# Probabilities of three attentions split to fp16 and turned by DMA; gate projections of the second layer moved ahead

## The chip, the cores and the metric

One of the eight cores of a Trainium2 chip runs the kernel. TensorE multiplies (the stationary operand is loaded first, the moving one streams past it) and writes PSUM; VectorE (DVE), ScalarE (ACT) and GpSimd (POOL) work on rows of 128 partitions; DMA queues move data between HBM and SBUF, or within SBUF. All DMAs of this kernel are issued in order from one queue, SyncE's (SP). The metric is the time of one execution on the device in microseconds; lower is better.

## What is computed

Two layers of a transformer trunk on a sequence of 1024 tokens with 1024 features. Each layer normalises `x`, projects it, runs two attentions, gates their outputs with `silu` of a gate projection, and projects back with a residual.

```python
def layer_ab(x, ...):            # A: top-256 of causal keys by an indexer; B: window of 128 with sinks
    oa = dsa_attention(qa, ka, va, qi, ki, wi, k_sel)
    ob = swa_sink_attention(qb, kb, vb, b_sinks)
    return x + concat([oa * silu(za), ob * silu(zb)]) @ w_out

def layer_cd(x, ...):            # C: compressed + selected + window 512, mixed by gates; D: latent attention
    oc = nsa_attention(qc, kc, vc, ks, vs, kw, vw, gates, n_sel)
    q  = (rms_norm(cq,  d_q_lat_norm)  @ d_w_uq)
    kv = (rms_norm(ckv, d_kv_lat_norm) @ d_w_ukv)
    od = mla_attention(q_nope, q_rope, k_nope, k_rope, kv_v)
    return x + concat([oc * silu(zc), od * silu(zd)]) @ w_out

def masked_softmax(s, mask):     # in every attention, before p @ v
    p = exp(s - max(s)); return p / sum(p)
```

Every attention has 8 heads in two groups of 4. A is the masked one: its mask comes from the top-k search.

## The kernel before

The sequence is cut into 8 blocks of 128 tokens. Products that need float32 accuracy are made from split operands: a high part and the rest, so that one product takes three matmuls (high x high, high x low, low x high). A projection chunk (`fill_gen`) is 256 columns of weights or a little more: for each of 8 blocks 8 x 3 matmuls (L490 to L492) run into a PSUM bank `pp`, and `post` evacuates it. Weights come by SP, ScalarE and GpSimd split them into `whi` and `wlo` (L446, L447); of the 14 buffer pairs a chunk uses 8, so 6 tiles are fetched ahead.

`attn_gen` runs a list of jobs, one for each block `i` and head group `g`. For `nk` keys, 4, 2 or 1 heads share one tile `pt` of up to 1024 columns: scores on TensorE into `psS` (L636), mask and running minimum of the negated scores on VectorE (L639), `exp` on ScalarE with the minimum `nm` as bias (L644). Then `tstage`, for four blocks of 128 columns at a time: TensorE turns the blocks (L664) into the PSUM tile `psT`, and the turned float32 probabilities are scaled by 4096 and split into two fp16 tiles `ph` and `pl`. The table `WAYS` says how, by attention and head group: in way `p` ScalarE writes `ph` (L668) and VectorE `pl` (L669), in way `q` ScalarE copies to `sg` (L673) and GpSimd does both (L674, L675). `cstage` multiplies with the values: three matmuls for each block (L682 to L684) into `po`; this is called P.V here. Transposes and P.V lag behind the scores by `tlag` groups.

C runs three kinds of jobs for each block and group (compressed keys `kcs`, selected `ks`, window `kw`), 52 tiles `pt` in a head group with 280 blocks of 128 columns; its first 24 jobs are head group 0, the next group 1. D has 44 tiles with 288 blocks, B 16 tiles with 120, A 44 tiles with 288.

`Lanes.run` interleaves a main list (attention) with a fill (projections): for each unit of cost that the main list yields, the fill may yield a ratio of it (`CR` for C, `DR` for D). The fill of C is the string `FOO`, the chunks of the second layer in order, followed by `d_prologue`, which prepares D: weights, keys, the first queries. `cq` (query latents) waits until group 0 of C is done. What the generators yield is the program's order; a scheduler then sets the final order of each engine.

Buffers that the steps touch: `pt` 3, `ph` and `pl` 4 each of four blocks, `sg` 2, `xr` (the residual of the last projection) 2, `wraw2` (raw weights of D and of the last projection) 2.

Of the kernel before, what the change touches and what calls it, by code (L numbers as in the profile page):

```python
# [38 lines left out]
PSCALE = 4096.0  # L39
SLOT = 2048  # L40
# [3 lines left out]
CR = 0.75  # L44
DR = 0.8
WB = 2
XB = 2
# [6 lines left out]
FOO = 'ks kc kw qc0 zc0 zc1 cq qc1 zd0 zd1 ck'  # L54
# [108 lines left out]
def trunk(ctx: ExitStack, tc: tile.TileContext, A, out):  # L163
# [165 lines left out]
    def tps():  # L329
        return psT.tile([P, 4, P], F32, name="psT")  # L330
# [202 lines left out]
    def v_scale(m, res):  # L533

        yield from L.take_in("psT", PTC)
        ps = tps()
        T.transpose(ps[0:1, 0], m, identf)
        yield
        r = st.tile([P, 2], F32, name="vs_r")
        V.tensor_reduce(r[0:1, 0:1], ps[0:1, 0], AX.X, OP.max)  # L540
        V.tensor_scalar(r[0:1, 0:1], r[0:1, 0:1], 2.0 ** -90, None, op0=OP.max)
        yield
        T.matmul(ps[:, 1, 0:1], r[0:1, 0:1].to_broadcast([1, P]), identf[0:1, 0:1], start=True, stop=True)
        yield
# [43 lines left out]
    def attn_gen(jobs):  # L588
# [9 lines left out]
        for jb in jobs:  # L598
# [22 lines left out]
            for h0 in range(0, 4, per):  # L621
# [33 lines left out]
                for c in range(0, len(todo), 4):  # L655
# [3 lines left out]
                    def tstage(jb=jb, grp=grp, pt=pt, lastg=lastg, vh=vh, vl=vl, nk=nk, get_po=get_po, fin=fin, cmp_=cmp_,  # L659
                               fb=fbox if h0 + per == 4 else None):  # L660
# [6 lines left out]
                        if next(jb["way"]) == "p":  # L667
                            S.activation(ph[:, :n], pT[:, :n], AF.Copy, scale=PSCALE)  # L668
                            V.scalar_tensor_tensor(pl[:, :n], pT[:, :n], PSCALE, ph[:, :n], op0=OP.mult,  # L669
                                                   op1=OP.subtract)  # L670
                        else:
                            sg = wk.tile([P, 4, P], F32, name="sg", bufs=SG)
                            S.activation(sg[:, :n], pT[:, :n], AF.Copy, scale=PSCALE)  # L673
                            G.tensor_scalar(ph[:, :n], sg[:, :n], 1.0, 1.0, op0=OP.mult, op1=OP.mult)  # L674
                            G.tensor_tensor(pl[:, :n], sg[:, :n], ph[:, :n], OP.subtract)  # L675
# [13 lines left out]
                        return cstage, n * 110  # L689
# [633 lines left out]
    def lat_pre():  # L1323
# [5 lines left out]
        B["glat"] = cc.tile([P, 384], F32, name="glat")  # L1329
        nc.sync.dma_start(B["glat"][:, 0:256], row(A["d_q_lat_norm"][0], 0, 256))  # L1330
        nc.sync.dma_start(B["glat"][:, 256:384], row(A["d_kv_lat_norm"][0], 0, 128))
# [3 lines left out]
    def lat_chain(z, ss, n, g, dst):  # L1335
# [3 lines left out]
        V.scalar_tensor_tensor(z, z, r[0], g, op0=OP.mult, op1=OP.mult)  # L1339
# [10 lines left out]
    def lat_start(ps, n, g, dst):  # L1350
# [5 lines left out]
        L.post(lat_chain(z[:, :n], ss, n, g, dst))  # L1356

    def cq_post(i, ps):
        t = slice(i * P, (i + 1) * P)
        lat_start(ps, 256, B["glat"][:, 0:256], (B["cqh"][:, :, t], B["cql"][:, :, t]))  # L1360
# [5 lines left out]
    def ck_post(i, ps):  # L1366
        t = slice(i * P, (i + 1) * P)
        lat_start(ps[:, 0:128], 128, B["glat"][:, 256:384], (B["ckh"][:, None, t], B["ckl"][:, None, t]))
# [78 lines left out]
    def small_w(ap, rows, n, tag):  # L1447
# [90 lines left out]
    def next_query():  # L1538
# [4 lines left out]
        if (i, g) == (0, 0):  # L1543
            D["wuq", 1] = small_w(wq[:, 384:768], 2, 384, "q")

    def d_prologue():
# [4 lines left out]
        D["wuq", 0] = small_w(wq[:, 0:384], 2, 384, "q")  # L1551
        D["wkv", 0] = small_w(wkv[:, 0:512], 1, 512, "kv")
        B["vscd"] = []
        L.post(v_bound(wkv, 1, B["glat"][:, 256:384], [], B["vscd"], ("vscd",)))
# [179 lines left out]
    D["wkv", 1] = small_w(wkv[:, 512:1024], 1, 512, "kv")  # L1734
# [63 lines left out]
```

## Time and profile before

| | us |
|---|---|
| three runs, median (lowest to highest) | 1560.41 (1559.73 to 1562.62) |
| the profiled execution | 1559.19 |
| its span, first to last instruction | 1557.4 |
| busy: TensorE, VectorE, ScalarE, GpSimd | 1384.3, 1226.1, 869.8, 821.4 |
| DMA: moved, busy share of the 16 engines | 93.19 MB, 20% |

The stages, by where the score matmuls of each attention stand in the trace: indexer scores to 168 us, B from 170 to 430, A from 428 to 636 (P.V included), projections alone to 839, C from 839 to 1226 (group 0 to 1038), D from 1264 to 1537, the last of the output after that. Shares over the whole span are means over stages with different limits, so the profile is read stage by stage: which engine is busy nearly all the time there, and which waits. A TensorE that is listed as busy may still hold a slow stream; its granted clock stands beside it.

### The profile page before, as it was taken

The page shows a single profiled execution, that of the slowest core. Times are in us where ns is not written, and L with a number is a line of the kernel's source. Part 1 is how long each engine was busy: PE and PEld are TensorE (multiplying, and loading weights), DVE is VectorE, ACT ScalarE, POOL GpSimd, SP SyncE. Part 2 cuts the span into 40 slices and gives each one's busy share as a digit, 9 for nine tenths or more (in the row PEclk, how much of TensorE's full clock was granted, in tenths as well). Part 3 has the DMA queues.
Part 4 walks back from the last instruction along what each step waited for, and adds up shares of the span by engine and source line. Part 5 has one row for each costly group of instructions (what it writes and reads, how often), then busy time and mean ns, then how long its engine had stood idle before and what let it go on. Part 6 is the DMA issues. An engine that isn't in the chain of part 4 may idle for free.

```text
span 1557.4 us, 35155 instructions
## 1 busy us (share of the span) xinstructions
PE 1384.3 (89%) x12588; PEld 1273.9 (82%) x12588; DVE 1226.1 (79%) x3827; ACT 869.8 (56%) x2385; POOL 821.4 (53%) x1097
## 2 busy tenths in 40 slices
PE   6998888788637889999999999999999778889999
PEld 6888878788636779999999998899988556778887
DVE  8599999999998876428338668976689999996763
ACT  6354576577406766325424666956667666754531
POOL 4767642467777657324447343565456565652240
PEclk9999999989867999999999999999999879989999
DMA  6311212111102132332312210012100210111232
GB/s 199 86 35 32 57 56 71 43 36 33 45 17 69 59 107 76 111 108 86 82 36 55 66 49 8 9 47 63 33 15 19 78 62 15 32 55 59 95 112 75
DMA packets 88431, 93.19 MB, mean 60 GB/s; under 512 B 20928, under 2 KB 73152, under 8 KB 88256
## 3 DMA queue, kind: packets, MB, share of 16 engines
q1 hardware_dynamic: 88256, 90.95, 19.3%
q8 instruction: 99, 1.62, 0.4%
q14 instruction: 76, 0.62, 0.1%
HBM read 67.85 MB, written 23.07 MB: 58 GB/s over the span
## 4 chain that ended last, share of the span: by engine, by line
PE 48%; DVE 33%; DMA 6%; POOL 5%; issue 5%; ACT 3%; SPq 0%; POOLq 0%; DVEq 0%; ACTq 0%
PE psS L636 8%; PE pp L490 7%; PE pp L492 6%; PE pp L491 6%; PE psT L664 6%; DVE junk L845 6%; DVE pt L639 4%; PE pp L1683 2%; PE pp L1681 2%; PE pp L1682 2%; PE po L684 2%; PE po L682 2%; PE po L683 2%; DMA wraw<-in_ab_w_in 1%; POOL wlo L447 1%
## 5 line engine op out<-in xcount | busy, mean ns | idle before, releaser
L490 PE MATMUL pp<-whi,Rh 128*128 128x256 f32 (+4 forms) x1648 | 489.1, 297 | 25.9 <-DVE zst L581 9.9
L492 PE MATMUL pp<-whi,Rl 128*128 128x256 f32 (+4 forms) x1648 | 481.0, 292 | 0.6 <-DVE Rl L327 0.6
L491 PE MATMUL pp<-wlo,Rh 128*128 128x256 f32 (+4 forms) x1648 | 480.0, 292 | 0.0
L490 PEld LDWEIGHTS pp<-whi,Rh 128*128 128x128 f32 x1648 | 322.5, 196 | 33.1 <-DVE zst L581 13.9
L644 ACT ACTIVATE pt<-pt,nm 128x256 f32<-128x256 f32 (+8 forms) x384 | 246.6, 643 | 178.6 <-DVE nm L639 173.3
L492 PEld LDWEIGHTS pp<-whi,Rl 128*128 128x128 f32 x1648 | 321.1, 195 | 2.2 <-DVE Rl L327 1.1
L491 PEld LDWEIGHTS pp<-wlo,Rh 128*128 128x128 f32 x1648 | 322.0, 196 | 1.0
L447 POOL TENSOR_TENSOR wlo<-wraw,whi 128x256 fp32r<-128x256 f32 (+4 forms) x208 | 162.3, 787 | 189.6 <-ACT whi L446 176.9
L664 PE MATMUL psT<-identf,pt 128*128 128x128 f32 x1256 | 216.1, 284 | 14.2 <-DVE pl L669 4.2
L674 POOL TENSOR_SCALAR ph<-sg 128x512 f16<-128x512 f32 (+3 forms) x157 | 89.3, 570 | 157.9 <-ACT sg L673 142.0
L664 PEld LDWEIGHTS psT<-identf,pt 128*128 128x128 f32 x1256 | 147.3, 143 | 28.1 <-issue 4.3
L675 POOL TENSOR_TENSOR pl<-sg,ph 128x512 f16<-128x512 f32 (+3 forms) x157 | 163.4, 1041 | 8.7
L446 ACT ACTIVATE whi<-wraw 128x256 fp32r<-128x256 f32 (+4 forms) x208 | 83.7, 416 | 125.0 <-DMA wraw<-in_cd_w_in 37.8
L669 DVE SCALAR_TENSOR_TENSOR pl<-psT,ph 128x512 f16<-128x512 f32 (+3 forms) x233 | 128.4, 556 | 26.8 <-ACT ph L668 26.4
L668 ACT ACTIVATE ph<-psT 128x512 f16<-128x512 f32 (+3 forms) x233 | 111.9, 492 | 51.7 <-PE psT L664 49.2
L684 PEld LDWEIGHTS <-pl 128*128 128x128 f16 x1256 | 114.2, 99 | 26.1 <-issue 7.4
L682 PEld LDWEIGHTS <-ph 128*128 128x128 f16 x1256 | 116.7, 100 | 20.0 <-issue 7.9
L683 PEld LDWEIGHTS <-ph 128*128 128x128 f16 x1256 | 116.7, 100 | 14.7 <-issue 13.5
L639 DVE CUSTOM_DVE_ANT_0 pt<-psS,mk 128x512 f32<-128x512 f32 (+4 forms) x208 | 107.1, 518 | 23.7 <-PE psS L636 21.8
L673 ACT ACTIVATE sg<-psT 128x512 f32<-128x512 f32 (+3 forms) x157 | 83.4, 534 | 32.7 <-PE psT L664 30.1
L344 POOL TENSOR_TENSOR nz<-nz,rs_y 128x512 f32<-128x512 f32 (+2 forms) x44 | 41.2, 937 | 94.0 <-DVE rs_y L288 68.2
L636 PE MATMUL psS<-ka,qs 128*128 128x512 f32 (+4 forms) x192 | 58.7, 405 | 24.1 <-DVE nm L639 23.8
(311 smaller groups left out, 3622.4 us busy)
## 6 DMA issues: line engine op xcount, KB each, us to landing
wraw<-in_cd_w_in SPq DMA_DIRECT2D x72, 128.0 KB, 2.1
wraw<-in_ab_w_in SPq DMA_DIRECT2D x56, 128.0 KB, 2.2
xs<-in_x SPq DMA_DIRECT2D x8, 512.0 KB, 6.0
od<-mx SPq DMA_DIRECT2D x32, 128.0 KB, 1.8
wraw<-in_ab_w_out SPq DMA_DIRECT2D x32, 128.0 KB, 2.2
x<-in_x SPq DMA_DIRECT2D x8, 512.0 KB, 4.6
mo<-od SPq DMA_DIRECT2D x16, 256.0 KB, 2.7
nz<-zdr SPq DMA_DIRECT2D x16, 256.0 KB, 2.8
```

What stands on the lines that cost most here:

```text
L447: G.tensor_tensor(lo[:, :o], raw[:, :o], hi[:, :o].bitcast(F32), OP.subtract)
L490: T.matmul(ps, xh, hi[:, :n], start=q == 0 and k == 0, stop=False)
L491: T.matmul(ps, xh, lo[:, :n], start=False, stop=False)
L492: T.matmul(ps, xl, hi[:, :n], start=False, stop=q == 3 and k == 1)
L636: T.matmul(ps[:, at + a - c:at + b - c], lhs, rhs(a, b), start=n == 0, stop=n == len(pl_) - 1)
L639: V.tensor_tensor_reduce(pt[:, j * nk + c:j * nk + c + w], ps[:, at:at + w], mask(c, w), -1.0, first, op0=OP.add, op1=OP.min, accum_out=low)
L644: S.activation(pt[:, j * nk:(j + 1) * nk], pt[:, j * nk:(j + 1) * nk], AF.Exp, scale=-1.0, bias=nm[:, h:h + 1], accum_out=sm[:, h:h + 1])
L664: T.transpose(pT[:, a], pt[:, o:o + P], identf)
L675: G.tensor_tensor(pl[:, :n], sg[:, :n], ph[:, :n], OP.subtract)
L682: T.matmul(dst, ph[:, a], vh(kt, h), start=kt == 0, stop=False)
L683: T.matmul(dst, ph[:, a], vl(kt, h), start=False, stop=False)
L684: T.matmul(dst, pl[:, a], vh(kt, h), start=False, stop=kt == nt - 1)
```

## The change

For B, C and D, `WAYS` now has the ways `g` and `d`, chosen once for a tile `pt`. The tile is split before it is turned: ScalarE copies it to fp16 (`hl`, first half), VectorE (`d`) or GpSimd (`g`) writes the rest into the second half, and one DMA on SP turns all blocks of both halves into `ht`, from which P.V takes its stationary operands. `hl` and `ht` have two buffers each. In A the ways `p` and `q` stay, chosen by tile too, and write into `ht`. The factor 4096 moves into the bias of `exp`: one more small ScalarE instruction on `nm` for each tile. In `FOO` the gate projections zd0 and zd1 move ahead of cq and qc1, and `CR` goes from 0.75 to 1.5; a turned tile's `tstage` counts 1 instead of 110 a block in the main list's cost. Besides, the latent norms' gains are multiplied into D's weights instead of the latents, and `xr` shares the two buffers of `wraw2`.

```diff
-CR = 0.75
+CR = 1.5
-XB = 2
-FOO = 'ks kc kw qc0 zc0 zc1 cq qc1 zd0 zd1 ck'
+FOO = 'ks kc kw qc0 zc0 zc1 zd0 zd1 cq qc1 ck'
+HLB = 2
+HTB = 2
-PHB = 4
-SG = 2
-WAYS = ('q', 'q', 'ppq', 'pq', 'ppq', 'pq', 'ppq', 'p')
+WAYS = ('g', 'g', 'ppq', 'pq', 'dg', 'dg', 'dgg', 'dg')
...
+                S.activation(nm[:, h0:h0 + per], nm[:, h0:h0 + per], AF.Copy, bias=LNP)
                 for j, h in enumerate(hs):
                     S.activation(pt[:, j * nk:(j + 1) * nk], pt[:, j * nk:(j + 1) * nk], AF.Exp, scale=-1.0,
                                  bias=nm[:, h:h + 1], accum_out=sm[:, h:h + 1])
+                way = next(jb["way"])
+                nb = per * nk // P
+                hts = []
+
+                def get_ht(hts=hts):
+                    if not hts:
+                        hts.append(wk.tile([P, 16, P], F16, name="ht", bufs=HTB))
+                    return hts[0]
+
+                if way in "dg":
+                    n = nb * P
+                    hl = wk.tile([P, 2048], F16, name="hl", bufs=HLB)[:, :2 * n]
+                    S.activation(hl[:, :n], pt[:, :n], AF.Copy)
+                    (V if way == "d" else G).tensor_tensor(hl[:, n:], pt[:, :n], hl[:, :n], OP.subtract)
+                    nc.sync.dma_start(get_ht()[:, :2 * nb], hl.rearrange("p (k n) -> p k n", n=P), transpose=True)
...
-                        pT = tps()
-                        for a, (h, kt, o) in enumerate(grp):
-                            T.transpose(pT[:, a], pt[:, o:o + P], identf)
-                        ph = wk.tile([P, 4, P], F16, name="ph", bufs=PHB)
-                        pl = wk.tile([P, 4, P], F16, name="pl", bufs=PHB)
...
+                        ht = get_ht()
+                        ph, pl = ht[:, c:c + n], ht[:, nb + c:nb + c + n]
+                        if way in "pq":
+                            pT = tps()
+                            for a, (h, kt, o) in enumerate(grp):
+                                T.transpose(pT[:, a], pt[:, o:o + P], identf)
...
-                        return cstage, n * 110
+                        return cstage, n * 110 if way in "pq" else 1
...
+            S.activation(raw, raw, AF.Copy, scale=B["glat"][:, g + r:g + r + 1])
...
-            xr = D["pool"].tile([P, 512], F32, name="xr", bufs=XB)
+            xr = D["pool"].tile([P, 512], F32, name="xr", tag="wraw2", bufs=WB)
```

How this moves instructions is shown at three places.

On TensorE, around the last scores of C (`kw`). Before, transposes of `pt` and the key projection of D (`whkv`, `wlkv`) stand around them:

```order
L664 MATMUL psT<-identf,pt 128x128 x2
L682 LDWEIGHTS ph
L682 MATMUL po<-vhs,ph 128x64
L683 LDWEIGHTS ph
L683 MATMUL po<-vls,ph 128x64
L1498 MATMUL pp<-whkv,Rh 128x256
L1499 MATMUL pp<-wlkv,Rh 128x256
L1500 MATMUL pp<-whkv,Rl 128x256
L636 MATMUL psS<-kw_10951,qs 128x320 x2
```

After (line numbers are those of the changed file):

```order
L699 LDWEIGHTS ht
L699 MATMUL po<-vhs,ht 128x64
L700 LDWEIGHTS ht
L700 MATMUL po<-vls,ht 128x64
L701 LDWEIGHTS ht
L701 MATMUL po<-vhs,ht 128x64
L637 MATMUL psS<-kw_10635,qs 128x320 x4
L637 MATMUL psS<-kd_16888,qhl 128x512 x2
L637 MATMUL psS<-krs,qrs 128x512
```

The transposes are gone, the operands of P.V come from `ht`, and the first scores of D (`kd`, `krs`) follow the last ones of C at once: the key projection for them stands earlier.

On SP, where the last projection chunk of C (160 columns, `ck`) is loaded. Before, the stores of gate projections (`zst`) are still going on:

```order
L442 DMA wraw<-in_cd_w_in 128x160 x3
L582 DMA zdr_102<-zst 128x256
L442 DMA wraw<-in_cd_w_in 128x160
L1295 DMA od_101<-cacc 128x256
L442 DMA wraw<-in_cd_w_in 128x160 x2
L582 DMA zdr_102<-zst 128x256
L442 DMA wraw<-in_cd_w_in 128x160 x2
```

After:

```order
L662 DMA_TRANSPOSE ht<-hl 128x16x128 x4
L662 DMA_TRANSPOSE ht<-hl 128x10x128 x2
L443 DMA wraw<-in_cd_w_in 128x160 x2
L662 DMA_TRANSPOSE ht<-hl 128x10x128 x2
L443 DMA wraw<-in_cd_w_in 128x160 x4
L1312 DMA od_101<-cacc 128x256
L443 DMA wraw<-in_cd_w_in 128x160
```

The gate stores stand earlier, as their chunks do, and transposing DMAs of 16 and 10 blocks stand between the loads.

On VectorE, near the beginning of D (`kd`, `krs`, `vdl`: keys and values of D). Before, `pl` comes in pieces of 512 columns for most tiles:

```order
L1488 TENSOR_TENSOR krs<-psT,krs 64x256
L639 ISA pt,nm<-psS,mk,nm_20436 128x384
L639 ISA nm 128x1
L669 SCALAR_TENSOR_TENSOR pl<-psT,ph 128x512
L278 TENSOR_SCALAR rs_y<-rs_v 128x8
L281 TENSOR_TENSOR rs_t<-rs_t,rs_v 128x8
L669 SCALAR_TENSOR_TENSOR pl<-psT,ph 128x512
L639 ISA pt,nm_20516<-psS,mk 128x512
L639 ISA nm_20516 128x1
```

After:

```order
L640 ISA pt,nm_19046<-psS,mk 128x512
L640 ISA nm_19046 128x1
L640 ISA pt,nm<-psS,mk,nm_19046 128x384
L640 ISA nm 128x1
L574 SCALAR_TENSOR_TENSOR vdl<-pp,vs_e,vdh 128x128 x2
L661 TENSOR_TENSOR hl<-pt,hl 128x1024
L640 ISA pt,nm_19113<-psS,mk 128x512
L640 ISA nm_19113 128x1
L574 SCALAR_TENSOR_TENSOR vdl<-pp,vs_e,vdh 128x128 x2
```

One subtraction of a whole tile (`hl`, 1024 columns) stands there for one tile, and none for its neighbours, whose way is `g`.

## Rows read from the trace of the kernel before

**Rows 1.** Busy time by stretch: its length, each engine (instructions), clock, DMA.

```profile
core 0: us, PE busy (x) PEld busy (x) DVE busy (x) ACT busy (x) POOL busy (x), PEclk, DMA share, GB/s
92.00:428.00 336.00, 276.72 (x2238) 263.15 (x2237) 328.49 (x937) 199.53 (x551) 195.14 (x245) 0.92 0.16 44
...
839.00:1038.00 199.00, 196.75 (x2136) 184.61 (x2135) 151.30 (x571) 131.24 (x386) 95.09 (x130) 1.00 0.14 38
1038.00:1203.00 165.00, 160.50 (x1782) 152.43 (x1782) 129.03 (x534) 107.86 (x340) 94.84 (x135) 1.00 0.11 32
1203.00:1264.00 61.00, 40.08 (x336) 32.63 (x335) 58.16 (x224) 39.21 (x118) 34.02 (x51) 0.78 0.22 68
1264.00:1400.00 136.00, 115.53 (x1011) 97.57 (x1011) 128.32 (x392) 92.19 (x237) 83.97 (x106) 0.91 0.14 43
1400.00:1557.00 157.00, 153.80 (x1177) 128.42 (x1175) 97.04 (x270) 61.74 (x152) 39.94 (x52) 1.00 0.26 85
```

**Rows 2.** Timeline of TensorE: start, duration, line, operands, count.

```profile
1132.89 0.93 PE L664 MATMUL psT<-identf,pt 128*128 128x128 f32 x7
1133.57 0.54 PE L636 MATMUL psS<-kw,qs 128*128 128x320 f32 x2
```

**Rows 3.** Busy time by stretch of the transposes alone (L664).

```profile
92.00:428.00 336.00, 22.79 (x120) 14.57 (x120) 0.92 0.16 44
839.00:1264.00 425.00, 97.17 (x560) 65.29 (x560) 0.97 0.14 40
1264.00:1400.00 136.00, 26.34 (x160) 18.89 (x160) 0.91 0.14 43
1400.00:1557.00 157.00, 20.76 (x130) 14.83 (x128) 1.00 0.26 85
```

**Rows 4.** Timeline of TensorE, last scores of C and first of D.

```profile
1225.48 0.45 PE L636 MATMUL psS<-kw,qs 128*128 128x320 f32 x2
1225.78 0.28 PE L1498 MATMUL pp<-whkv,Rh 128*128 128x256 f32 x1
1225.90 0.28 PE L1499 MATMUL pp<-wlkv,Rh 128*128 128x256 f32 x1
...
1264.12 1.91 PE L636 MATMUL psS<-kd,qhl 128*128 128x512 f32 x4
```

**Rows 5.** Busy time by stretch of VectorE's `pl` alone (L669).

```profile
1038.00:1264.00 226.00, 24.55 (x47) 0.94 0.14 42
1264.00:1400.00 136.00, 18.31 (x31) 0.91 0.14 43
1400.00:1557.00 157.00, 23.94 (x41) 1.00 0.26 85
```

**Rows 6.** Groups by shape: count, busy us, mean ns, idle before.

```profile
L516 DVE SCALAR_TENSOR_TENSOR pt<-x,rs_y,gx 128x1024 f32<-128x1024 f32 x8 | 10.3, 1294 | 0.2
L510 ACT ACTIVATE pt<-x 128x1024 f32<-128x1024 f32 x8 | 8.5, 1059 | 1.7 <-DVE x L1091 1.7
L675 POOL TENSOR_TENSOR pl<-sg,ph 128x512 f16<-128x512 f32 x38 | 44.6, 1175 | 2.7
L715 ACT ACTIVATE es<-es 128x4 f32<-128x4 f32 x16 | 3.1, 196 | 4.2 <-DVE es L713 4.2
```

**Rows 7.** Busy time by stretch of VectorE's gates alone (L581).

```profile
1038.00:1264.00 226.00, 6.61 (x16) 0.94 0.14 42
```

**Rows 8.** DMA issues: operands, count, KB each, us to landing.

```profile
mo<-od SPq DMA_DIRECT2D x16, 256.0 KB, 2.7
x1d<-x SPq DMA_DIRECT2D x8, 512.0 KB, 3.0
xs<-in_x SPq DMA_DIRECT2D x8, 512.0 KB, 6.0
rope<-in_c_rope SPq DMA_DIRECT2D x1, 256.0 KB, 7.5
```

**Rows 9.** Waits of SP's queue: us in total, times, longest.

```profile
SPq L442 <- POOL wlo L447: 363.3, 160, 27.8
```

More of the change, by code (lines that the diff above doesn't have):

```diff
@@ L39 @@
 PSCALE = 4096.0
+LNP = float(np.log(PSCALE))
+HLB = 2
+HTB = 2
 SLOT = 2048
@@ L657, in attn_gen, with tstage @@
                     lastg = h0 + per == 4 and c + 4 >= len(todo)
-                    def tstage(jb=jb, grp=grp, pt=pt, lastg=lastg, vh=vh, vl=vl, nk=nk, get_po=get_po, fin=fin, cmp_=cmp_,
-                               fb=fbox if h0 + per == 4 else None):
+                    def tstage(grp=grp, pt=pt, lastg=lastg, vh=vh, vl=vl, nk=nk, get_po=get_po, fin=fin, cmp_=cmp_,
+                               fb=fbox if h0 + per == 4 else None, way=way, get_ht=get_ht, nb=nb, c=c):
                         n = len(grp)
-                        pT = tps()
-                        for a, (h, kt, o) in enumerate(grp):
-                            T.transpose(pT[:, a], pt[:, o:o + P], identf)
-                        ph = wk.tile([P, 4, P], F16, name="ph", bufs=PHB)
-                        pl = wk.tile([P, 4, P], F16, name="pl", bufs=PHB)
[L667 to L675, printed above, removed]
@@ new lines, in tstage @@
+                        ht = get_ht()
[4 more added lines that the diff above has]
+                                T.transpose(pT[:, a], pt[:, o:o + P], identf)
+                        if way == "p":
+                            S.activation(ph, pT[:, :n], AF.Copy)
+                            V.tensor_tensor(pl, pT[:, :n], ph, OP.subtract)
+                        elif way == "q":
+                            sg = wk.tile([P, 4, P], F32, name="sg", tag="hl", bufs=HLB)
+                            S.activation(sg[:, :n], pT[:, :n], AF.Copy)
+                            G.tensor_scalar(ph, sg[:, :n], 1.0, 1.0, op0=OP.mult, op1=OP.mult)
+                            G.tensor_tensor(pl, sg[:, :n], ph, OP.subtract)
@@ L1328, in lat_pre, with lat_chain @@
         D["kx"] = ks_[:, 1024:2048].rearrange("p (a b n) -> p a b n", a=2, b=2)
-        B["glat"] = cc.tile([P, 384], F32, name="glat")
-        nc.sync.dma_start(B["glat"][:, 0:256], row(A["d_q_lat_norm"][0], 0, 256))
-        nc.sync.dma_start(B["glat"][:, 256:384], row(A["d_kv_lat_norm"][0], 0, 128))
+        B["glat"] = cc.tile([P, 3], F32, name="glat")
+        nc.sync.dma_start(B["glat"][:, 0:2], A["d_q_lat_norm"][0].rearrange("(k p) -> p k", p=P))
+        nc.sync.dma_start(B["glat"][:, 2:3], A["d_kv_lat_norm"][0].rearrange("(k p) -> p k", p=P))
         G.tensor_scalar(B["glat"], B["glat"], RG, 1.0, op0=OP.mult, op1=OP.mult)
-    def lat_chain(z, ss, n, g, dst):
+    def lat_chain(z, ss, n, dst):
         yield
@@ L1348, in lat_chain, with lat_start @@
         L.give("psT")
-    def lat_start(ps, n, g, dst):
+    def lat_start(ps, n, dst):
         L.take("nz", NZ)
@@ L1445, in wout_gen, with small_w @@
                     yield
-    def small_w(ap, rows, n, tag):
+    def small_w(ap, rows, n, tag, g):
         hi = D["pool"].tile([P, rows, n], F32R, name="wh" + tag)
@@ L1543, in next_query @@
         if (i, g) == (0, 0):
-            D["wuq", 1] = small_w(wq[:, 384:768], 2, 384, "q")
+            D["wuq", 1] = small_w(wq[:, 384:768], 2, 384, "q", 0)
     def d_prologue():
@@ L1550, in d_prologue @@
         D["kd"] = [D["pool"].tile([P, 2, SEQ], F32R, name=f"kd{n}") for n in range(2)]
-        D["wuq", 0] = small_w(wq[:, 0:384], 2, 384, "q")
-        D["wkv", 0] = small_w(wkv[:, 0:512], 1, 512, "kv")
+        D["wuq", 0] = small_w(wq[:, 0:384], 2, 384, "q", 0)
+        D["wkv", 0] = small_w(wkv[:, 0:512], 1, 512, "kv", 2)
         B["vscd"] = []
-        L.post(v_bound(wkv, 1, B["glat"][:, 256:384], [], B["vscd"], ("vscd",)))
+        L.post(v_bound(wkv, 1, B["glat"][:, 2:3], [], B["vscd"], ("vscd",)))
         for i0 in range(0, NT, 2):
@@ L1733, in trunk @@
             L.tick()
-    D["wkv", 1] = small_w(wkv[:, 512:1024], 1, 512, "kv")
+    D["wkv", 1] = small_w(wkv[:, 512:1024], 1, 512, "kv", 2)
     FD = d_fill()
```

10 lines of the change are left out of this document (5 added, 5 removed).

## Prediction

> **What bounds the kernel now.** I read the busy time by stretch first [rows 1]: it cuts the span into stages with different limits. From 92 to 428 us VectorE is busy 328 of 336 us (the top-k search, with attention B beside it), so TensorE, busy 277, has slack. From 839 to 1203 us, attention C, TensorE is busy 357 of 364 us at the full clock while VectorE has 77%: TensorE is the limit. From 1203 to 1264 us it turns round: VectorE 58 of 61 us, TensorE 40 at a granted 0.78. That is the hand-over to attention D: keys, queries and values are prepared, and between the last score matmul of C at 1225.5 and the first of D at 1264.1 TensorE gets none [rows 4]. VectorE still leads to 1400 us (128 of 136), and then TensorE does to the end (154 of 157).
>
> So a transpose taken off TensorE is worth its time in C and after 1400 us, and nothing where VectorE leads; a VectorE instruction is the other way round.
>
> **What goes.** 968 transposes (L664): 120 of B, 560 of C, 288 of D (two stand on the border of the last two stretches) [rows 3]; the 288 of A stay. Seven in a row start 0.68 us before the next matmul starts [rows 2], 97 ns each: 280 x 0.097 = 27 us of TensorE in each half of C (head groups 0 and 1), and 130 x 0.097 = 12.6 us after 1400 us [rows 3]. The evacuations `ph`, `sg` and their scaling go too.
>
> **What comes.** For each tile `pt` of B, C and D: one ScalarE copy to fp16, one subtraction (VectorE or GpSimd, by `way`), one transposing DMA on SP's queue, and a small ScalarE instruction that shifts the bias. The tile's bytes: C has 560 blocks of 128 columns in 104 tiles, so a mean of 689 columns; both halves in fp16 make 345 KB. Prices: the copy 689/1024 of 1059 ns = 0.71 us; the subtraction 689/1024 of 1294 ns = 0.87 us on VectorE or 689/512 of 1175 ns = 1.58 us on GpSimd, by turns, 1.23 us on average; the bias 0.2 us [rows 6].
>
> The transposing DMA has no row. The nearest plain ones land 2.7 us after issue for 256 KB and 3.0 to 6.0 us for 512 KB [rows 8]. Between 2.7 and the middle 4.5, 345 KB comes to 3.3 us; the low end, towards 3.0, is 2.8. A far bound is the rope table, a load in pieces of 256 bytes, which is also what one row of a 128-column block holds: 7.5 us for 256 KB, so 10.1 us for 345. I take 3.3, since the rope load stood at the program's start behind 512 KB loads, and keep 10.1 for the range. The Trainium skill is of two minds. "Advanced Engine Details and Errata" (X-Bar Transpose) holds transposing DMAs to be as fast as plain ones on this chip: with that 3.3 us stands, and so does the sum. "VectorE: DVE Perf Modes" (The three transpose paths) gives 1309 ns for one 128x128 block by DMA and prefers TensorE wherever PSUM will do; that is the first rival's rule. No row here shows either.
>
> **How much cover it has.** `hl` and `ht` have two buffers each. One `hl` is held through copy, subtraction and DMA: 0.71 + 1.23 + 3.3 = 5.2 us, so a tile every 2.6 us, 137 us for the 52 tiles of one head group. While that is below the stage's other bound it costs nothing. The new order of TensorE shows the cover: while projections last, some eighty of them (0.118 us each, [rows 4]) and other tiles' matmuls stand between a tile's scores and its P.V matmuls, ten microseconds or so.
>
> **C, group 0** (839 to 1038 us, 199). TensorE-bound. It loses 27 us of transposes, but the order of loads shows that zd0 and zd1 now run here: 2 chunks x 8 tiles x 24 matmuls at 0.118 us (successive starts, [rows 4]) = 45 us. Net +18: 217 us. The `hl` cycle's 137 us stays below.
>
> **C, group 1, and the hand-over** (1038 to 1264 us, 226). TensorE loses 27 + 45 us of the 200 it was busy and is no longer the limit. VectorE was busy 129 + 58 = 187 us. It loses 6.6 us of gates [rows 7] and 24.6 of `pl` [rows 5]; it gets half of 280 x 128 columns, 17920 x 1.264 ns = 22.6 us. Left: 178. ScalarE, 147 busy, swaps evacuations for copies of the same columns and gains 52 x 0.2 = 10 us; GpSimd's 129 fall, since its fp16 copies go. VectorE is the limit, and the preparation of D, which in the new order of TensorE is done before C's last scores, fills the gaps it had. At the 95% that it reached from 1203 to 1264 us: 187 us, 39 less. If the chain leaves it at the 83% it has over these 226 us now, nothing of the 39 comes: second rival.
>
> **D** (1264 to the end). `pl` costs VectorE 18.3 us before 1400 [rows 5] and 42.3 in all of D. The new way gives it a third of group 0 and half of group 1, 15360 columns x 1.264 = 19.4 us, 46%. So -10 us in the VectorE-bound part and -12.6 of transposes in the TensorE-bound part: -23. D's tiles are larger (44, mean 838 columns; 419 KB by the same line is 3.8 us): copy 0.87, subtraction 1.56, a tile every 3.1 us, 137 us of 293: hidden.
>
> **Nothing at A and B.** B's transposes go, but VectorE sets the pace there and its subtractions were on GpSimd before as after. A keeps its transposes; its way is now chosen by tile instead of by four blocks, and each tile has the 0.2 us bias step in its chain: within 6 us either way. Latent gains folded into the D weights add one small scaling per row block; hidden behind C. `xr` now shares two buffers with the weight loads; both are needed after 1400 us, but by then all but the last of them are in.
>
> **SP's queue** runs in order. The transposes wait on GpSimd or VectorE and on `ht`, so weight loads and stores of gates queue behind them, and they behind weight loads, which already wait for `wlo` 160 times [rows 9]. With three microseconds at a time, and weights fetched six tiles ahead, I cost it at nothing; without that cover it joins the DMA's latency in the `hl` cycle.
>
> **Sum.** +18 - 39 - 23 = -44 us. The profiled execution took 1559.2 us (span 1557.4), 1.2 below the median 1560.4; so 1515 against it, 1516 against the median.
>
> **Rivals.**
> 1. *The transposes by DMA are slow.* With t for a mean tile of C, a group takes 26 x (1.94 + t). That passes 187 us at t = 5.3 and 217 at 6.4, and the whole gain is gone at about 6.7, where both groups take 225. At t = 8 each takes 258: C costs 113 us more than forecast and D stays covered, 1629. At 10.1: 313 each, and D's 44 tiles at 7.4 us are 323 instead of 270, together about 1790. For it: pieces of 256 bytes, an in-order queue, two buffers. Against: the plain rows, all under 4.6 us at 345 KB and below save rope's. By the 1309 ns of the skill's page, 10.8 halves of blocks would make 14 us a tile, an estimate beyond all of these. 0.27, most of it between 1565 and 1650.
> 2. *The wait moves, and group 1 keeps its time.* Without projections to fill, TensorE stands at each P.V for the chain mask, bias, exp, copy, subtraction, DMA, some 9 us with only two tiles in flight, and VectorE waits for its scores. Then -39 is 0: 1559 + 18 - 23 = 1554. For it: in the new order four fifths of group 1's tiles have hardly a projection left between them. Against: the cycle sum above. 0.15.
> 3. *TensorE's whole saving comes through.* If VectorE's preparation spreads into group 0 as well, C and D lose 850 x 0.097 = 82 us: 1477. For it: VectorE has 48 us idle in group 0. Against: queries and keys of D need latents that are projected last. 0.10.
>
> That the transposes don't leave TensorE is excluded: 288 are left in the new order.
>
> **Chances.** Forecast (1490 to 1540) 0.48; rivals as above. Faster by over 0.2%, about what a measurement of this kernel can tell from none: 0.48 + 0.10 and half of the second, 0.66; same 0.06; slower 0.28. The range runs from 1465, which takes in rival 3, to 1620, which takes in the slow side up to t just under 8; above it I leave some 0.13, below 0.04.
>
> **What would show it.** Transposes landing 2.8 to 4.6 us after issue, group 0 some 18 us longer with TensorE above 95%, group 1 with VectorE above 90%, no gap between the last score of C and the first of D, 288 transposes left. Wrong: P.V matmuls waiting for DMA `ht<-hl` as the longest wait of TensorE in C (rival 1; rival 2 if the landing is short), or fp16 copies waiting for it on `hl`.

## The result, and the profile after

The changed kernel takes 1613.2 us (median of four runs, 1608.9 to 1621.8) against 1561.5 before: 1.0338 times as long, 95% interval 1.0293 to 1.0383. Forecast were 1516 us, and at most 1620. The profiled execution's span is 1612.1 us.

Stages are cut here at the first score matmul of C, of its second head group, and of D:

| stage | before | forecast | after |
|---|---|---|---|
| up to C | 839 | 839 | 837 |
| C, group 0 | 199 | 217 | 244 |
| C, group 1, and the hand-over to D | 226 | 187 | 219 |
| D, to the end | 293 | 270 | 312 |

Busy time by stretch of the changed kernel (columns as in [rows 1]; these are group 0, group 1, D):

```profile
core 0: us, PE busy (x) PEld busy (x) DVE busy (x) ACT busy (x) POOL busy (x), PEclk, DMA share, GB/s
837.00:1082.00 245.00, 223.08 (x2285) 210.26 (x2283) 160.91 (x558) 148.88 (x433) 102.79 (x114) 0.96 0.62 123
1082.00:1300.00 218.00, 160.87 (x1325) 132.79 (x1323) 168.65 (x694) 141.50 (x428) 99.53 (x105) 0.72 0.52 108
1300.00:1612.00 312.00, 251.29 (x1980) 206.72 (x1980) 220.78 (x625) 159.93 (x400) 143.47 (x145) 0.91 0.54 122
```

Where [rows 1] showed TensorE busy 357 of 364 us in C at the full clock, it now stands still 22 us in group 0 and, with the hand-over, 57 in group 1, there at a granted clock of 0.72. The same two stages had 2 and 25 us of stands before (199 and 226 us less the busy times of [rows 1]). VectorE, which I had expected to take over, is at 77% in group 1. Nothing leads: each engine waits for another. The waits of group 1 (who <- for whom: us, times, longest):

```profile
PEld psS L637 <- DVE nm L640: 44.2, 56, 3.4
POOL hl L661 <- ACT hl L660: 31.9, 13, 5.0
PEld L699 <- DMA ht<-hl: 30.8, 25, 3.9
PE psS L637 <- DVE nm L640: 30.5, 37, 3.3
...
PE po L699 <- DMA ht<-hl: 22.9, 16, 3.6
ACT hl L660 <- DMA ht<-hl: 21.0, 19, 3.2
...
DVE pt L640 <- POOL hl L661: 15.9, 8, 3.4
```

P.V (L699) waits for the turned tile, and ScalarE's fp16 copy (L660) for the DMA that still reads the `hl` it wants. TensorE's longest wait is another: for VectorE (L640), which takes the scores out of PSUM and so makes room for the next ones (30.5 us, against 11.3 in the run order_only below). VectorE itself stood 15.9 us there until GpSimd had subtracted, because the buffer of `pt` that it wants is read until then. The DMA itself is not slow (operands, count, median us to landing; beside it the plain load that [rows 8] listed at 2.7):

```profile
mo<-od SPq DMA_DIRECT2D x16, 256.0 KB, 3.0
...
ht<-hl SPq DMA_TRANSPOSE x164, 3.9
```

The gap of [rows 4] between C's last scores and D's first is gone, as forecast (starts of 1298.7 and 1300.5):

```profile
1298.71 0.83 PE L637 MATMUL psS<-kw,qs 128*128 128x320 f32 x4
1300.54 1.19 PE L637 MATMUL psS<-kd,qhl 128*128 128x512 f32 x2 [1.00 <-DVE nm L640]
```

The mechanism can be read off ScalarE's row of events (start, duration, line, operands, idle before and what ended it):

```profile
1241.22 0.19 ACT L644 ACTIVATE nm<-nm 128x1 f32<-128x1 f32 x1
1241.44 0.83 ACT L646 ACTIVATE pt<-pt,nm 128x640 f32<-128x640 f32 x1
1242.18 0.19 ACT L646 ACTIVATION_READ_ACCUMULATOR pt<-pt,nm 128x1 f32 x1
1245.00 0.74 ACT L660 ACTIVATE hl<-pt 128x640 f16<-128x640 f32 x1 [2.64 <-DMA ht<-hl]
1245.65 0.19 ACT L644 ACTIVATE nm<-nm 128x1 f32<-128x1 f32 x1
1245.93 0.83 ACT L646 ACTIVATE pt<-pt,nm 128x640 f32<-128x640 f32 x1
```

TensorE's beside it:

```profile
1245.03 0.20 PE L699 MATMUL po<-vhs,ht 128*128 128x64 f16 x1 [2.77 <-DMA ht<-hl]
1245.12 0.19 PE L699 MATMUL po<-vhs,ht 128*128 128x64 f16 x1
1245.21 0.19 PE L699 MATMUL po<-vhs,ht 128*128 128x64 f16 x1
1245.31 0.24 PE L699 MATMUL po<-vhs,ht 128*128 128x64 f16 x1
1245.46 0.24 PE L699 MATMUL po<-vhs,ht 128*128 128x64 f16 x1
```

and the row of VectorE in which the next tile's minimum is ready:

```profile
1244.22 0.08 DVE L640 DVE_READ_ACCUMULATOR2_ANT nm<- 128x1 f32 x1
```

One landing, just before 1245, releases both. ScalarE has stood 2.64 us at the copy; for the last 0.7 us of that the next tile's minimum was there (1244.30), but its bias step and exp (1245.65, 1245.93) stood behind the copy in order. TensorE has stood 2.77 us, and soon after runs at half its clock: successive blocks (three matmuls each) are 0.09 us apart at 1245.1 and 0.15 from 1245.3 on.

### The profile page after: what moved, and what is told of

It is laid out like the page before. It is cut to its first block, busy times and chain, and to the rows that moved or that the text cites. A ratio compares the mean times of both kernels' runs of the same rounds, so it can differ in the third digit from the quotient of the medians.

```text
span 1612.1 us, 33283 instructions
## 1 busy us (share of the span) xinstructions
PE 1333.1 (83%) x11620; PEld 1207.9 (75%) x11620; DVE 1204.4 (75%) x3715; ACT 896.1 (56%) x2459; POOL 786.2 (49%) x948
## 2 busy tenths in 40 slices
DMA packets 341608, 156.34 MB, mean 97 GB/s; under 512 B 274368, under 2 KB 326336, under 8 KB 341440
## 5 line engine op out<-in xcount | busy, mean ns | idle before, releaser
L661 POOL TENSOR_TENSOR hl<-pt,hl 128x1024 f16<-128x1024 f32 (+5 forms) x93 | 156.0, 1678 | 215.7 <-ACT hl L660 174.9
L448 POOL TENSOR_TENSOR wlo<-wraw,whi 128x256 fp32r<-128x256 f32 (+4 forms) x208 | 156.9, 765 | 194.9 <-ACT whi L447 189.3
L699 PEld LDWEIGHTS <-ht 128*128 128x128 f16 x1256 | 123.9, 106 | 95.6 <-DMA ht<-hl 76.3
L660 ACT ACTIVATE hl<-pt 128x1024 f16<-128x1024 f32 (+5 forms) x164 | 136.0, 831 | 59.8 <-DMA ht<-hl 58.4
L640 DVE CUSTOM_DVE_ANT_0 pt<-psS,mk 128x512 f32<-128x512 f32 (+4 forms) x208 | 107.0, 522 | 55.5 <-PE psS L637 35.9
L644 ACT ACTIVATE nm<-nm 128x1 f32<-128x1 f32 (+2 forms) x208 | 41.7, 201 | 166.5 <-DVE nm L640 166.0
L701 PEld LDWEIGHTS <-ht 128*128 128x128 f16 x1256 | 125.0, 106 | 11.1 <-POOL ht L692 4.0
L700 PEld LDWEIGHTS <-ht 128*128 128x128 f16 x1256 | 125.5, 106 | 4.1 <-issue 3.4
L661 DVE TENSOR_TENSOR hl<-pt,hl 128x640 f16<-128x640 f32 (+4 forms) x71 | 67.0, 943 | 22.4 <-ACT hl L660 22.2
L637 PEld LDWEIGHTS psS<-ka,qs 128*128 128x128 f32 x192 | 32.6, 211 | 59.2 <-DVE nm L640 58.8
L637 PE MATMUL psS<-ks,qs 128*128 128x512 f32 (+4 forms) x192 | 64.9, 437 | 11.7 <-DVE nm L640 11.5
L637 PE MATMUL psS<-kd,qhl 128*128 128x512 f32 (+4 forms) x192 | 58.4, 386 | 19.0 <-DVE nm L640 15.7
```

What stands on the lines that cost most here:

```text
L448: G.tensor_tensor(lo[:, :o], raw[:, :o], hi[:, :o].bitcast(F32), OP.subtract)
L637: T.matmul(ps[:, at + a - c:at + b - c], lhs, rhs(a, b), start=n == 0, stop=n == len(pl_) - 1)
L640: V.tensor_tensor_reduce(pt[:, j * nk + c:j * nk + c + w], ps[:, at:at + w], mask(c, w), -1.0, first, op0=OP.add, op1=OP.min, accum_out=low)
L660: S.activation(hl[:, :n], pt[:, :n], AF.Copy)
L661: (V if way == "d" else G).tensor_tensor(hl[:, n:], pt[:, :n], hl[:, :n], OP.subtract)
L699: T.matmul(dst, ph[:, a], vh(kt, h), start=kt == 0, stop=False)
```

## The experiments

Theory 1: the DMA way makes the chain from a tile's scores to its P.V longer (bias step, copy, subtraction, issue, landing), and where it isn't covered TensorE stands and its granted clock falls. Against it stand the order of the projections (2), the two buffers of `hl` and `ht` (3) and the clock by itself (4).

Stage lengths in us from the profiled execution of each; medians of the timed runs; the ratio is to the kernel before in the same session, whose median lay between 1557.6 and 1562.1. A profiled execution can lie up to 11 us from the median of its kernel, so differences of stages don't add up to differences of medians.

| run | median | ratio (95%) | C starts | group 0 | group 1 | D |
|---|---|---|---|---|---|---|
| before | 1561.5 | 1 | 839 | 199 | 226 | 293 |
| changed | 1613.2 | 1.034 (1.029 to 1.038) | 837 | 244 | 219 | 312 |
| order_only | 1578.8 | 1.011 (1.009 to 1.013) | 840 | 242 | 198 | 300 |
| dma_only | 1612.5 | 1.032 (1.030 to 1.034) | 836 | 224 | 251 | 300 |
| D_turned_on_TensorE | 1618.1 | 1.036 (1.032 to 1.039) | 834 | 243 | 222 | 310 |
| C_turned_on_TensorE | 1577.9 | 1.010 (1.007 to 1.013) | 837 | 245 | 194 | 300 |
| lag_two_tiles | 1606.8 | 1.031 (1.028 to 1.035) | 836 | 241 | 221 | 307 |
| four_small_buffers | 1606.9 | 1.031 (1.027 to 1.035) | 840 | 246 | 218 | 307 |
| half_the_bytes_turned | 1571.6 | 1.009 (1.006 to 1.011) | 847 | 236 | 199 | 299 |
| filler_transposes | 1660.5 | 1.066 (1.063 to 1.068) | 835 | 269 | 227 | 327 |
| three_hl | 1625.9 | 1.044 (1.040 to 1.047) | 852 | 231 | 205 | 344 |
| small_weights | 1651.1 | 1.059 (1.056 to 1.062) | 847 | 245 | 206 | 351 |
| changed_no_bias_step | 1596.8 | 1.026 (1.023 to 1.029) | 835 | 240 | 214 | 306 |

### Order or turning, C or D

```diff
# order_only: the kernel before with
+CR = 1.5
+FOO = 'ks kc kw qc0 zc0 zc1 zd0 zd1 cq qc1 ck'
# dma_only: the changed kernel with
+CR = 0.75
+FOO = 'ks kc kw qc0 zc0 zc1 cq qc1 zd0 zd1 ck'
# D_turned_on_TensorE, C_turned_on_TensorE: the changed kernel with
+WAYS = ('g', 'g', 'ppq', 'pq', 'dg', 'dg', 'ppq', 'p')
+WAYS = ('g', 'g', 'ppq', 'pq', 'ppq', 'pq', 'dgg', 'dg')
```

> The kernel before with the new order of the projections alone (zd0, zd1 ahead of cq; CR 1.5); every transpose stays on TensorE. Theory 1 (the DMA way makes the chain from a tile's scores to its P.V matmuls longer, and where no projections stand in it TensorE waits and its granted clock falls): little waiting here; group 0 of C 240 to 250 us (199 before, plus two chunks of 24 us), group 1 with the hand-over 185 to 205 (226 before), D 290 to 296: 1555 to 1585. Theory 2 (the order costs it: group 1 has lost its cover, however P is turned): group 1 stays at 215 to 226 and the time is 1595 to 1615.

> The changed kernel with the old order and ratio (FOO, CR 0.75); transposes of B, C and D by DMA. Theory 1: the second half of group 0 and the last of group 1 have no projections now, so TensorE waits for ht there; group 0 205 to 225 us, group 1 with the hand-over 225 to 245, D 305 to 315: 1585 to 1615. Theory 2: with projections in group 1 again the transposes' saving shows, group 0 172 to 180, group 1 about 200, D 305: 1530 to 1560.

> The changed kernel, but D's probabilities are turned on TensorE again (its ways as before). Theory 1: D from its first scores to the end comes back from 312 to 290 to 300 us, C stays at 463: 1592 to 1602, and TensorE's clock in D is again 0.93 or more. Rival for D (its loss is from the residual's shared buffers and the scaled weights, not from the turning): D stays at 308 to 314, 1608 to 1616.

> The changed kernel, but C's probabilities are turned on TensorE again (its ways as before), with the new order. Theory 1: C as with the new order alone, 425 to 450 us from its first scores to D's first, clock above 0.9 up to the end of the projections; D 312: 1575 to 1600. Theory 2 (the order): C stays at 455 to 465, 1605 to 1615.

The order alone costs 17 us by the medians. In the profiled executions, which lie 22 apart, the two chunks make group 0 43 us longer, group 1 with the hand-over gives back 29, D takes 7. C's turning by DMA costs 35 us beside the new order (1577.9 to 1613.2) and 37 beside the old one (1575.8, old_order_C_on_TensorE below, to 1612.5, dma_only). So the loss in C goes with the turning, as theories 1 and 3 have it, and theory 2 falls. For D theory 1 falls: turned on TensorE again, D stays at 310, and turned by DMA with C on TensorE it takes the same 300 us as with all on TensorE. The number of its rival came out, the cause did not: C_turned_on_TensorE has the shared residual buffers and the scaled weights too, and its D is as long as that of order_only, which has neither. My forecasts for D missed in order_only (290 to 296), dma_only (305 to 315) and C_turned_on_TensorE (312): it took 300 each time. The stretches of order_only show what group 1 would be with the transposes on TensorE:

```profile
839.00:1082.00 243.00, 240.50 (x2510) 231.53 (x2509) 161.42 (x588) 143.23 (x417) 103.50 (x144) 1.00 0.17 48
1082.00:1279.00 197.00, 168.34 (x1672) 145.39 (x1672) 172.54 (x724) 135.90 (x418) 127.94 (x175) 0.87 0.12 37
```

TensorE does 347 matmuls more in group 1 than in the changed kernel, in 21 us less, and VectorE is at 88%.

### Chain, buffers, bytes or clock

```diff
# lag_two_tiles, for C and D
-        return (n + 3) // 4
+        return 2 * ((n + 3) // 4)
# four_small_buffers: split and turned by four blocks
-                    hl = wk.tile([P, 2048], F16, name="hl", bufs=HLB)[:, :2 * n]
+                    for c in range(0, nb, 4):
+                        hl = wk.tile([P, 1024], F16, name="hl", bufs=2 * HLB)[:, :2 * n]
-                        hts.append(wk.tile([P, 16, P], F16, name="ht", bufs=HTB))
+                        hts[c] = wk.tile([P, 8, P], F16, name="ht", bufs=2 * HTB)
# half_the_bytes_turned
-  dma_start(get_ht()[:, :2 * nb], hl.rearrange(...), transpose=True)
+  dma_start(get_ht()[:, :nb], hl[:, :n].rearrange(...), transpose=True)
...
+                        if way in "dg":
+                            pl = ph
# filler_transposes: for each tile of C and D
+                                for a in range(8):
+                                    T.transpose(pj[:, a % 4], identf, identf)
```

> The changed kernel with P.V of C and D two tiles behind the scores in the program's order instead of one; buffers stay two. Theory 1 (the chain from scores to P.V is longer than what stands between them on TensorE): TensorE's 76 us of waits for ht fall below 30, and the clock of group 1 rises from 0.72 to above 0.85: 1560 to 1590. Theory 3 (the two buffers of hl and ht limit the rate): the waits move to scores and to the fp16 copies, 1600 to 1620.

> The changed kernel with the split and the turning done for each four blocks of 128 columns instead of a tile: hl and ht have four buffers of half the size, so the same bytes, and a piece is at most 256 KB. More copies, subtractions and DMAs for it. Theory 3 (buffers): ScalarE's 58 us of waits for the turning DMA fall below 25 and the time to 1570 to 1595. Theory 1: the first piece of a tile lands about 1 us earlier, of 9, so 1595 to 1610. If the number of DMAs on SP's queue limits: slower, 1620 to 1650.

> The changed kernel, but the DMA turns the high half of each tile alone; P.V reads it in place of the low half too, so this part of the result is left out. All copies and subtractions stay. The landing should fall from 3.9 to about 2.7 us. Theories 1 and 3 (every microsecond of landing is exposed in about two tiles of three of C): 96 tiles of 164 x 1.2 us x 0.7 = 80 us at most, half of that with two in flight: 1570 to 1595. If the DMA's length isn't what costs (issue on SP, the longer work of ScalarE): 1600 to 1613.

> The changed kernel with eight transposes of the identity on TensorE for each tile of C and D that nothing reads, 0.78 us each time at the full clock (96 tiles, 75 us of work in all). If the lower granted clock is a large part of the loss (theory 4): the clock of group 1 rises from 0.72 to above 0.9 and the time is 1590 to 1615 in spite of the added work. If only the waits count: the work adds to them by half, 1635 to 1660.

With half the bytes the landing falls from 3.9 to 3.0 us and 42 us of the 52 come back by the medians (31 in the profiled execution, the slowest of its five); ScalarE hardly stands at the copies any more (47 us in C before this edit, 3.5 after), and group 1 is at 199, close to the 198 of order_only. But the edit takes out more than bytes. The DMA no longer reads what the subtraction writes, so it doesn't wait for it. A tile of the changed kernel (rows as above; x2 is two issues, of which the first is this tile's):

```profile
1140.07 0.85 ACT L660 ACTIVATE hl<-pt 128x768 f16<-128x768 f32 x1
1141.08 1.64 POOL L661 TENSOR_TENSOR hl<-pt,hl 128x768 f16<-128x768 f32 x1
1142.75 7.11 SPq L662 DMA_TRANSPOSE ht<-hl  x2
```

and one of this run, issued 0.03 us after the copy, with the subtraction behind it:

```profile
1137.54 0.84 ACT L660 ACTIVATE hl<-pt 128x768 f16<-128x768 f32 x1
1138.41 1.21 SPq L662 DMA_TRANSPOSE ht<-hl  x1
1140.05 1.71 POOL L661 TENSOR_TENSOR hl<-pt,hl 128x768 f16<-128x768 f32 x1
```

Over the tiles of C (copies paired in order with the issues and landings, means), a copy's end comes 1.94 us before the issue in the changed kernel and 0.32 us here; from issue to landing it is 3.81 and 3.00. So a tile's way from copy to landing is 2.4 us shorter, of which two thirds are the wait for the subtraction and one third the DMA. The length of this way is what costs; that the DMA's own length does, this run doesn't show by itself.

A P.V one more tile behind gave 6 us by the medians and 4 by the ratios, and the two intervals overlap. It doesn't test what it was meant to: the program's order has P.V later, TensorE's final order hardly does. Counted from the matmuls of C, 22.5 blocks of 128 columns on the mean have been scored and not yet multiplied when a P.V matmul of group 1 starts, in both kernels (18.9 and 19.5 in group 0). So theory 1 in the form that P.V simply stands too close behind its scores is neither shown nor refuted. Four small buffers gave as little: a piece lands sooner (3.2 us), but there are more of them, and ScalarE still stood 39 us at the copies of C.

Eight useless transposes a tile, ahead of its P.V, raise the clock of group 1 from 0.72 to 0.86, and of the 40 us they add there (52 tiles x 8 x 0.097) only 8 show; over the whole kernel they cost 47. TensorE's busy time grows by 23 us there, not by 40, so its other work took some 17 us less, an estimate of what the clock gave back, and the stage is still 8 us longer. The 1660.5 us lie just above what I had named for the case that only the waits count. The low clock is not the root of the loss; whether it is a part of it, this run doesn't show. The row of group 1 with the filler is

```profile
1104.00:1330.00 226.00, 183.57 (x1770) 161.32 (x1769) 176.52 (x700) 142.96 (x432) 99.84 (x108) 0.86 0.52 105
```

### A third buffer

```diff
# three_hl; small_weights is the same without the first line
+HLB = 3
+WBF = 12
+WB = 1
```

> The changed kernel with three buffers of hl instead of two; for their room the weight buffers fall from 14 to 12 and wraw2 (with the residual) to one. To be read against the next run, which has the smaller weight buffers alone. Ring theory (ScalarE stands at the fp16 copy until the turning DMA of two tiles earlier has landed, and the exps of the next tile stand behind it): ScalarE's 58 us of waits for the DMA fall below 20, C (first scores of C to first scores of D) is 20 to 35 us shorter than in the run beside it. Chain theory (P.V one tile behind its scores): C within 8 us of it.

> The control for three buffers of hl: the changed kernel with 12 weight buffers instead of 14 and one wraw2 instead of two, hl at two. All theories: C within 10 us of the changed kernel's 463, D longer by 5 to 25 since residual and output weights now share one buffer: 1615 to 1640.

Read against its control, the third `hl` brings 25 us by the medians (1651.1 to 1625.9) and 16 in the profiled executions; there 15 lie in C, 14 of them in group 0. Waits for the turning DMA in C, with two buffers (small_weights):

```profile
ACT hl L660 <- DMA ht<-hl: 43.0, 40, 3.6
PEld L699 <- DMA ht<-hl: 36.1, 35, 2.7
```

and with three:

```profile
PEld L699 <- DMA ht<-hl: 37.0, 35, 4.5
...
ACT hl L660 <- DMA ht<-hl: 4.6, 7, 1.8
```

ScalarE's stand is gone, TensorE's is not. So the ring is one cause, in group 0; the 15 us lie between the two theories (20 to 35, and within 8). In group 1 the third buffer gave 1 us, so the ring isn't the limit there, and that leaves the serial chain. The smaller weight buffers cost 38 us, more than the third buffer gives and more than I had forecast: D is 39 us longer, with one buffer for weights and residual. C of the control is 12 us shorter than in the changed kernel (within 10 forecast), and that lies in group 1; why is open.

### A link of the chain: the bias step

```diff
# changed_no_bias_step
-                S.activation(nm[:, h0:h0 + per], nm[:, h0:h0 + per], AF.Copy, bias=LNP)
```

> The changed kernel without the bias step and with it without the factor 4096. The step stands in the chain from scores to P.V that the DMA way has made critical, so here it should cost more than the 3 us it cost with C on TensorE: 164 tiles x 0.3 us (the step and a hop), 49 us at most, a third of it exposed: 1590 to 1603. If chains don't count and only the rate of the hl ring does: 1608 to 1613.

One ScalarE instruction of 0.2 us a tile is worth 12 us (by the ratios) to 16 (by the medians) where C goes by DMA, as expected. Its durations (ns: least, median, most), first and last start, and shapes:

```profile
L644 ACT ACTIVATE nm<-nm x208: 187/204/270, 180.3 to 1585.5; 128x1 f32<-128x1 f32 x65, 128x4 f32<-128x4 f32 x21, 128x2 f32<-128x2 f32 x18
```

### What is left in the old order, and a better version

All of these are the changed kernel with the old `FOO` and `CR`; B and D go by DMA unless it says "all".

| run, all with old_order_ ahead | median | ratio (95%) | C starts | group 0 | group 1 | D |
|---|---|---|---|---|---|---|
| C_half_by_DMA | 1611.5 | 1.033 (1.032 to 1.035) | 835 | 219 | 258 | 295 |
| C_on_TensorE | 1575.8 | 1.010 (1.008 to 1.012) | 836 | 205 | 237 | 297 |
| all_on_TensorE | 1583.8 | 1.016 (1.014 to 1.018) | 850 | 205 | 238 | 294 |
| C_on_TensorE_small_buffers | 1570.5 | 1.009 (1.006 to 1.012) | 842 | 204 | 233 | 289 |
| C_on_TensorE_no_bias_step | 1572.9 | 1.009 (1.006 to 1.011) | 842 | 201 | 227 | 301 |
| C_on_TensorE_small_buffers_no_bias_step | 1551.6 | 0.9965 (0.9951 to 0.9980) | 828 | 201 | 228 | 290 |
| all_on_TensorE_small_buffers_no_bias_step | 1569.5 | 1.006 (1.004 to 1.009) | 845 | 202 | 228 | 294 |

```diff
# WAYS with the old order
# C_on_TensorE:  ('g', 'g', 'ppq', 'pq', 'ppq', 'pq', 'dgg', 'dg')
# all_on_TensorE: ('q', 'q', 'ppq', 'pq', 'ppq', 'pq', 'ppq', 'p')
# C_half_by_DMA: ('g', 'g', 'ppq', 'pq', 'dpgq', 'dpgq', 'dgg', 'dg')
# small_buffers and no_bias_step: the edits of four_small_buffers and changed_no_bias_step
```

> The changed kernel with both suspects undone: the old order and ratio of the projections, and C's probabilities turned on TensorE; B and D still by DMA. If order (17 us) and C's turning account for the whole loss: 1553 to 1565. If something else of the change costs (bias step, ways by tile, shared residual buffers): 1570 to 1580.

> The changed kernel with the old order and every other tile of C turned by DMA, the others on TensorE, so that the two hl buffers have twice the time. Ring theory: no stand at the copies, C shorter than before by some of the 27 us of transposes taken away: 1540 to 1558. Chain theory: every tile by DMA still stands before its P.V: 1575 to 1595.

> The changed kernel with the old order and every probability turned on TensorE, so that only the rest of the change is left: the bias step, the way by tile, ht of whole tiles in two buffers, sg in hl's buffers, shared residual buffers. If the rest is what keeps the old order with C on TensorE 17 us above the kernel before: 1570 to 1582. If it is D's and B's turning by DMA: 1556 to 1564.

> As the old order with C on TensorE, but ht and hl in four buffers of four blocks, as ph and pl had before. If the two whole-tile buffers cost the 17 us (P.V of a tile must end before the evacuations of the tile after next begin): 1556 to 1566. If the bias step or the way by tile does: 1572 to 1580.

> As the old order with C on TensorE, without the ScalarE instruction that shifts the bias of exp; the factor 4096 is left out with it. It stands between the minimum and the exps of each tile, some 0.2 us and one more hop of 148 tiles in B, C and D and 44 in A. If this is the 17 us: 1556 to 1566. If buffers or ways: 1570 to 1578.

> The old order with C on TensorE, with the small buffers and without the bias step (and the factor) together: if the two (5 and 3 us) add up, 1565 to 1570, and 6 to 11 us over the kernel before are left for the way by tile and the rest. If they hide each other: 1570 to 1573; if they were both limits of the same chain: 1556 to 1564.

> The old order, small buffers, no bias step (and no factor), and every probability turned on TensorE, B and D too: the kernel before but for the way by tile, the scaled weights and the shared residual buffers. To be read against the run with C alone on TensorE (1551.6). If B's and D's turning by DMA is what brings that one under the kernel before, 8 us as with the large buffers: 1557 to 1563. If the rest of the change does, 1548 to 1554.

Order and C's turning undone together still leave 17 us, so I had missed something. With no tile turned by DMA at all it is even 26: the rest of the change, which I had costed at nothing, is dear, and turning B by DMA pays part of it back. Neither the bias step alone (3 us by the medians) nor the small buffers alone (5) is clear of noise, though in the profiles C is 14 us shorter without the step and D 8 us with the small buffers. The two together bring 24 by the medians and 21 by the ratios; in the profiles 13 lie in C and 7 in D. They also moved the start of C from 836 to 828, though each alone had moved it to 842; why is open. Of the seven expectations, those for C_on_TensorE and for the bias step alone named the range that came; the other five runs fell outside all of theirs.

That version, 1551.6 us (without the factor 4096), beats both kernels: 0.35% under the kernel before, in one session. The last run says in part what it owes this to. With B and D turned on TensorE it is 18 us slower (15 by the ratios), and 17 of them are there when C starts. The first scores of C, with all on TensorE:

```profile
844.98 0.30 PE L637 MATMUL psS<-kcs,qs 128*128 128x64 f32 x2
```

and with B and D by DMA:

```profile
828.25 0.30 PE L637 MATMUL psS<-kcs,qs 128*128 128x64 f32 x2
```

From 3 to 4 of these 14 (850 to 836) and 17 us are there before B's first scores, so B's turning brings 10 to 13. That is against B in way `q` within the changed kernel; in the kernel before, B's first scores and C's first lie 669 us apart, as in old_order_C_on_TensorE, and 663 in the better version. So turning by DMA pays in B when nothing else is changed, is even in D (within 4 us either way: 310 on TensorE and 312 by DMA, 294 and 297, 294 and 290), and costs 35 in C. Half of C's tiles by DMA was no better than all of them: for the tiles of way `q`, `sg` lies in the same ring, and ScalarE stood 23.9 us at it for those DMAs; where the rest went is open.

## Why the prediction was wrong, step by step

- **The bound of before** was read rightly: in order_only, two chunks more in a group 0 where TensorE leads cost 43 us (45 forecast).
- **The landing** was nearly right: 3.3 us forecast for a tile of C, 3.7 measured (the median there; 3.9 over all, 2.4 at least, 7.2 at most). Rival 1 came near in time (1629) but not in cause; it needed 8 us. The Trainium skill, "VectorE: DVE Perf Modes" (The three transpose paths), whose 1309 ns a block made 14 us a tile, is not borne out: no landing was above 7.2. The Trainium skill, "Advanced Engine Details and Errata" (X-Bar Transpose), which holds transposing DMAs to be as fast as plain ones, is: 3.7 us for 345 KB on the mean lies between the plain 3.0 for 256 KB and 3.0 to 5.9 for 512 KB.
- **"While that is below the stage's other bound it costs nothing"** is the step that failed, in C: the turning that it costs at nothing beside the saving of 27 us a group costs 35 net. The size was off too: over C one `hl` is held 6.5 us, not 5.2 (the copy 0.78 for 0.71, from its end to the issue 1.94 for 1.23, the landing 3.8 for 3.3, means). But 26 x 6.5 is 170 us, still below the 187 forecast for group 1, so it is the rule that failed. From 837 to 1000, with 6.2 us a tile and a tile every 4.5 us, 1.36 of two buffers are in use on the mean, and that looks like cover. But tiles come in bursts: both buffers are in use half of that time, and ScalarE stood 17.7 us at copies. A stand of ScalarE, which works in order, also stops the exp of the next tile and with it VectorE and TensorE. From 1200 to 1300, where a tile comes every 3.3 us, 1.87 of two are in use, yet a third buffer gave group 1 only 1 us: what is left there is each tile's chain itself, from its scores to its P.V, which is argued and not shown. A mean cycle against a mean stage says nothing of stands.
- **Group 0**: -27 was forecast for the transposes. They left TensorE, and 22 us of standing and a clock of 0.84 from 1000 to 1050 took their place: 244 with the DMA, 242 without.
- **Group 1 and the hand-over**: the order alone brought 29 of the 39, and the gap closed. The DMA way took 21 back. This is near rival 2 (stands at P.V and VectorE short of work), at a chance of 0.15; I had it in group 1 alone. Which link of its chain counts how much is not shown.
- **D**: -23 forecast, +18 measured. Its turning is worth nothing instead of 23. The new order alone gives +7: the evacuations of D's values (`vdh`), of which 13 of 28 came ahead of D's first scores before, come behind them there but for one; that this is the cause is not shown. C's turning in the old order gives +3 (dma_only against old_order_C_on_TensorE), the two together +18, with D on TensorE as well (D_turned_on_TensorE, +17). 18 P.V matmuls of C now stand behind D's first scores; how the 18 us arise is open.
- **Nothing at A and B** was right only as a sum: B by DMA brings 10 to 13 us, and the rest of the change costs about as much there (all_on_TensorE starts C at 850).
- **The bias step**, "0.2 us", was costed by its duration beside an idle engine. It stands in the chain of each tile, and is worth 12 to 16 us in the changed kernel.
- **The signs.** The landing, the closed gap and the 288 transposes left came as forecast. Group 0 grew by 45 us instead of 18, with TensorE at 91% and VectorE in group 1 at 77%, where I had named 95% and 90%. The sign of being wrong is there: fp16 copies stood 46.6 us in C for the DMA that reads `hl`.

In short, I summed the engines' loads, while what the change lengthened was the latency from scores to P.V. That C's turning costs 35 us is shown, and so is that most of the loss goes when the way from copy to landing is 2.4 us shorter, with half the bytes. How it divides between ring, chain and clock is not: the third `hl` gives 16 to 25 beside the smaller weight buffers, the bias step 12 to 16, and they overlap.

## What to carry to other kernels

Moving work from a busy engine to a DMA trades throughput for latency: before costing the DMA at nothing, draw one tile from its scores to its last use, put each link in, and look how many tiles the buffers and the in-order queues let fly at once. A buffer ring that is two thirds used on the mean (1.36 of two, in group 0) can already stall, and the stall lands on whatever engine issues the next write to it. Where another engine leads and there is slack (B here), the same edit did no harm; try it stage by stage. And look in the trace whether a test changed what it was meant to: the deeper lag left TensorE's order as it was, and half the bytes took a wait away with them.

## What was not expected of the hardware

A transposing DMA holds its queue far longer than a plain one: SP is 1.46 us at the issue (median), against 0.33.

```profile
L662 SPq DMA_TRANSPOSE ht<-hl x164: 1188/1457/3607, 190.3 to 1589.4; - x164
```

```profile
L443 SPq DMA_DIRECT2D wraw<-in_cd_w_in x88: 327/328/1826, 681.9 to 1034.5; - x88
```

And it is moved in small packets: under 512 B there are 274368 of 341608 now, against 20928 of 88431 before, and the DMA engines' mean busy share in group 0 is 0.62, against 0.14 in [rows 1].
